# The RG-LRU block of a hybrid trunk: the square of the decay is taken out of the input's factor, and z's tiles get five buffers

## The chip, the core and the metric

The kernel runs on one core of a Trainium2 chip. The core has four engines that compute: TensorE (PE in the profile; its weight loads are listed as PEld), VectorE (DVE), ScalarE (ACT) and GpSimd (POOL). A fifth, SyncE (SP), only issues transfers here. Transfers run on 16 DMA engines and are issued from the queues of SP, ACT and POOL, each of which works in order. The metric is the device time of one execution in microseconds (us); lower is better.

## What is computed

Two layers of a trunk with 512 latent tokens and 256 context tokens, all in float32. The change lies in layer 0, whose mixer has two halves: SSD heads (Mamba-2) and RG-LRU blocks. The part of the reference that matters is the RG-LRU scan, which is done for two directions and eight blocks of 128 channels:

```python
def rglru_scan(u, h0, w_a, b_a, w_i, b_i, lam):
    r = jax.nn.sigmoid(jnp.einsum("btnk,nkj->btnj", u, w_a) + b_a)
    i = jax.nn.sigmoid(jnp.einsum("btnk,nkj->btnj", u, w_i) + b_i)
    log_a = -LRU_C * jax.nn.softplus(-lam) * r
    a = jnp.exp(log_a)
    bx = jnp.sqrt(-jnp.expm1(2 * log_a)) * (i * u)
    h = linear_recurrence(a, bx, h0)
    return h, h[:, -1]
...
y = rms_norm(y * jax.nn.silu(p["z"]), ssd_norm_g)
r = lru_h.reshape(bsz_, t, LRU_W) * jax.nn.gelu(p["gy"])
```

The factor sqrt(1 - a^2) is never formed from 1 - a^2 in the kernel. With c = 8 softplus(-lam), so that a = exp(-c r), the kernel before uses 1 - a^2 = (1 + a^2) tanh(c r), and the changed one uses 1 - a^2 = (1 + a)^2 tanh(c r / 2).

## The kernel before

Activations lie with channels on the 128 partitions and T = 768 tokens along the free dimension, context first. Every projection is done in three passes on TensorE, with weights and inputs split into a high and a low part: ScalarE writes the high part of a weight panel (`whi`, in `whalf`, L185 to L193), VectorE the low part (`wlo`, L193), in two halves of a panel.

The change touches one stage, `lru_phase` (L1236 to L1335). It works through eight blocks n of 128 channels. For each n there are these steps, written as a generator in an order of its own (L1316 to L1321):

- `proj_u(n)` (L1239): the projection of u, 24 matmuls of 512 columns into a `px` tile and 24 of 256 columns into a `pc` tile; then a causal convolution (`conv1d`), one tap on ScalarE and three on VectorE, and the split of the result into `uhi` and `ulo`.
- `proj_g(n)` (L1252): the projection of the output gate, in the same form, and a GELU on ScalarE that reads `px` and `pc` and writes `ge`.
- `gates(n)` (L1262): four products with 128x128 weights (`ghi`, `glo`) and a sigmoid each, which ScalarE writes into four tiles of the tag `gate` (four buffers): r and i for the two directions.
- `recur(n)` (L1285): for both directions a = exp(-c r) into `la_`, tanh(c r) in place; then the square of a into a tile `a2` that has one buffer, and (1 + a^2) tanh on VectorE (L1298); then the square root on ScalarE, two products, and the scan over time on VectorE (L1306 to L1309). The products i u (L1302) and the sum of the directions (L1311) run on GpSimd. The product with `ge` (L1312) is VectorE's, and the result goes out to `r_d`.
- `z_panel(n // 2)` for odd n (L1223): 256 columns of z. Six chunks of 128 tokens, each of 24 matmuls of 256 columns into a tile `pz`, which has the tag and the two buffers of `pc`. ScalarE copies `pz` to `zt`, which has two buffers, and issues the transfer of `zt` to `z_d`.

Between the steps run two other strands: the SSD scan (`ssd_phase`; its tiles are `bc`, `xw`, `yi`, `pyi`, `pin`, `pst`, `pcbm`), and the modulation vectors of later layers (`mod_tick`: tiles `mst` and `macc`, products on VectorE). The order in which each engine issues its instructions is not that of the program's text alone: the framework that the kernel is written in orders them over all engines from the dependences and its own estimates, so an edit can move instructions that it does not name.

ScalarE holds one table of functions at a time; where the next function needs another, an `ACT_TABLE_LOAD` stands in its queue.

Of the kernel before, what the change touches and what calls it, by code (L numbers as in the profile page):

```python
# [9 lines left out]
F32 = mybir.dt.float32  # L10
F32R = mybir.dt.float32r
AF = mybir.ActivationFunctionType
ALU = mybir.AluOpType
# [4 lines left out]
T = 768  # L18
# [46 lines left out]
def build(tc, I, out, dbg=None):  # L65
    nc = tc.nc
    V, S, G, PE, SP = nc.vector, nc.scalar, nc.gpsimd, nc.tensor, nc.sync
    if dbg is not None and "wrap" in dbg:
        V, S, G, PE, SP = [dbg["wrap"](e, n) for e, n in ((V, "V"), (S, "S"), (G, "G"), (PE, "PE"), (SP, "SP"))]
# [9 lines left out]
    def act(o, i, f, bias=0.0, scale=1.0, **kw):  # L79
        return S.activation(o, i, f, bias=bias, scale=scale, **kw)  # L80

    def stt(o, a, s, b, op0, op1, eng=None):
        return (eng or V).scalar_tensor_tensor(o, a, s, b, op0=op0, op1=op1)  # L83
# [5 lines left out]
    def psc(name="pc", n=256):  # L89
        return pp.tile([128, n], F32, tag="pc", name=name, bufs=2)  # L90
# [4 lines left out]
    def dump(name, ap):  # L95
        if dbg is not None and name in dbg:
            SP.dma_start(dbg[name], ap)
# [76 lines left out]
    def PS(n, i, k):  # L174
        q = POFF[n] + i
        assert q // 128 == (q + k - 1) // 128
        return PAR[q // 128][:, q % 128:q % 128 + k]
# [25 lines left out]
    def wpanel(W, r0, kt, c0, n, gain=None, byk=False, eng=None):  # L203
        return wsplit(wload(W, r0, kt, c0, n), kt, n, gain, byk, eng)
# [13 lines left out]
    def mm3s(o, hh, sl, w):  # L218

        for k in range(8):  # L220
            whi, wlo = w[k // 4]
            PE.matmul(o, hh[k][0][:, sl], whi[:, k % 4, :], start=(k == 0), stop=False)  # L222
            PE.matmul(o, hh[k][0][:, sl], wlo[:, k % 4, :], start=False, stop=False)  # L223
            PE.matmul(o, hh[k][1][:, sl], whi[:, k % 4, :], start=False, stop=(k == 7))  # L224
# [457 lines left out]
    def softplus_pos(dst, src, e, z, z2, p_):  # L682

        act(e, src, AF.Abs)
        act(e, e, AF.Exp, scale=-1.0)
        V.tensor_scalar(z, e, 2.0, None, op0=ALU.add)
        V.reciprocal(z, z)
        V.tensor_mul(z, z, e)
        V.tensor_mul(z2, z, z)
        V.tensor_scalar(p_, z2, 1.0 / 17, 1.0 / 15, op0=ALU.mult, op1=ALU.add)  # L690
        for m in (13, 11, 9, 7, 5, 3, 1):
            V.tensor_mul(p_, p_, z2)
            V.tensor_scalar(p_, p_, 1.0 / m, None, op0=ALU.add)
        V.tensor_mul(p_, p_, z)
        V.tensor_scalar(z2, src, 0.0, None, op0=ALU.max)
        stt(dst, p_, 2.0, z2, ALU.mult, ALU.add)
# [517 lines left out]
    c8 = ssc.tile([128, 16], F32, name="c8")  # L1214
    c8n = ssc.tile([128, 16], F32, name="c8n")
    with tc.tile_pool(name="c8p", bufs=1, reuse_waits="tile") as c8p:
        tt = [c8p.tile([128, 16], F32, name=f"c8t{i}") for i in range(5)]
        V.tensor_scalar(tt[4], PS("lam", 0, 16), -1.0, None, op0=ALU.mult)
        softplus_pos(c8, tt[4], tt[0], tt[1], tt[2], tt[3])
        V.tensor_scalar(c8n, c8, -8.0, None, op0=ALU.mult)  # L1220
        V.tensor_scalar(c8, c8, 8.0, None, op0=ALU.mult)

    def z_panel(lp, pb):  # L1223

        w = wpanel(W0, 0, 8, pb * 256, 256, byk=True, eng=G if KG[4] else V)
        for c in range(6):
            ps = psc("pz")
            cs = slice(c * 128, (c + 1) * 128)
            mm3s(ps, h, cs, w)
            zt = lp.tile([128, 256], F32, tag="zt", name="zt", bufs=2)  # L1230
            act(zt, ps, AF.Copy)
            S.dma_start(z_d[c, :, pb * 256:(pb + 1) * 256], zt)
            if c % 2:
                yield

    def lru_phase(lp):  # L1236
# [48 lines left out]
        def recur(n, u, gate):  # L1285
            hs, as_ = [], []
            for d in range(2):
                r_ = gate[d]
                ci = d * 8 + n
                a_ = lp.tile([128, T], F32, tag="la", name="la_", bufs=2)  # L1290
                act(a_, r_, AF.Exp, scale=c8n[:, ci:ci + 1])
                act(r_, r_, AF.Tanh, scale=c8[:, ci:ci + 1])
                as_.append(a_)
            for d in range(2):
                r_, a_ = gate[d], as_[d]
                a2 = lp.tile([128, T], F32, tag="la2", name="a2", bufs=1)
                act(a2, a_, AF.Square)
                stt(r_, a2, 1.0, r_, ALU.add, ALU.mult)  # L1298
            for d in range(2):
                r_, i_, a_ = gate[d], gate[2 + d], as_[d]  # L1300
                act(r_, r_, AF.Sqrt)
                (G, V)[d < KG[15]].tensor_mul(i_, i_, u)  # L1302
                (V, G)[d < KG[14]].tensor_mul(i_, i_, r_)
                h_ = r_
                if d == 0:
                    V.tensor_tensor_scan(h_, a_, i_, 0.0, op0=ALU.mult, op1=ALU.add)  # L1306
                else:
                    V.tensor_tensor_scan(h_[:, 0:256][:, ::-1], a_[:, 0:256][:, ::-1], i_[:, 0:256][:, ::-1], 0.0, op0=ALU.mult, op1=ALU.add)
                    V.tensor_tensor_scan(h_[:, 256:768][:, ::-1], a_[:, 256:768][:, ::-1], i_[:, 256:768][:, ::-1], h_[:, 0:1], op0=ALU.mult, op1=ALU.add)  # L1309
                hs.append(h_)  # L1310
            (V, G)[KG[0]].tensor_add(hs[0], hs[0], hs[1])  # L1311
            (V, G)[KG[1]].tensor_mul(hs[0], hs[0], GE.pop(n))  # L1312
            SP.dma_start(r_d[n], hs[0])
            dump(f"r_{n}", hs[0])
# [7 lines left out]
        for s_, n in order:  # L1322
            if s_ == "u":
                proj_u(n)
                yield
            elif s_ == "g":
                proj_g(n)
            elif s_ == "c":
                g_ = gates(n)
                yield  # L1330
                recur(n, *g_)
                yield
            else:
                yield from z_panel(lp, n // 2)
# [778 lines left out]
```

## Time and profile before

| | |
|---|---|
| time, median of 3 runs | 2139.82 us (2135.62 to 2142.2) |
| the profiled execution's own time | 2138.01 us |
| span from first to last instruction in it | 2136.3 us |
| mean granted TensorE clock | 0.975 of full speed |
| PE busy | 2022.4 us, 95% of the span |
| DVE busy | 1571.1 us, 74% |
| ACT busy | 872.8 us, 41% |
| POOL busy | 273.0 us, 13% |
| the stage of the RG-LRU | from about 240 to 560 us |

The profile gives times in us from the span's start. A row of a timeline has the start, the duration, the engine, the line of the kernel, the operation, the tiles written and read, and in brackets how long the engine stood idle just before and what released it. Helpers record many operations at one line: L80 is any activation, L83 any scalar_tensor_tensor, L215 any matmul of a projection. A table of windows gives for each stretch the busy time of the engines, and as PEclk the clock that TensorE was granted (1.00 is 2.4 GHz, 0.50 is 1.2 GHz).

### The profile page before, as it was taken

To read this page: it belongs to the slowest core of one execution; us is meant where nothing else is said; L and a number is where in the kernel's file an instruction comes from. 1 tells how busy PE (TensorE), PEld (TensorE's weight loads), DVE (VectorE), ACT (ScalarE), POOL (GpSimd) and SP (SyncE) were. 2 spreads that over 40 slices of the span, in tenths; PEclk is the share of its full clock that TensorE was granted. 3 is DMA by queue.
4 is the path that set the end of the run, shared out by engine and by line. 5 is a ranking of instruction groups with operands and counts; after the bars stand their busy time and mean duration, and the time that the engine had idled before them with its cause. 6 is when DMAs were issued, how large, how long until landed. Compare 5 with 4: busy or idle time off the path is not lost.

```text
span 2136.3 us, 32686 instructions
## 1 busy us (share of the span) xinstructions
PE 2022.4 (95%) x12738; PEld 1699.5 (80%) x12738; DVE 1571.1 (74%) x2916; ACT 872.8 (41%) x1276; POOL 273.0 (13%) x234
## 2 busy tenths in 40 slices
PE   8969989898898999999999999999999899999998
PEld 4848778787677888888888888897877688888887
DVE  5898898767778888868765656656876678667484
ACT  4625577586533442212321323324444344223234
POOL 2142333344421000000000000110011100000000
PEclk9979899999999999999999999999999999999999
DMA  9437535435676322333234112554421123222321
GB/s 332 132 102 206 152 98 168 123 97 165 225 242 215 99 87 94 112 121 116 94 118 139 62 50 94 152 160 147 126 71 58 40 80 99 97 82 98 99 84 55
DMA packets 283019, 261.09 MB, mean 122 GB/s; under 512 B 23406, under 2 KB 263061, under 8 KB 282865
## 3 DMA queue, kind: packets, MB, share of 16 engines
q1 hardware_dynamic: 257504, 243.35, 35.8%
q10 hardware_dynamic: 24464, 13.75, 2.3%
q8 instruction: 100, 1.64, 0.3%
q0 software_dynamic: 896, 1.90, 0.2%
q14 instruction: 55, 0.44, 0.1%
HBM read 224.17 MB, written 34.78 MB: 121 GB/s over the span
## 4 chain that ended last, share of the span: by engine, by line
PE 62%; DVE 6%; DMA 4%; POOL 1%; issue 1%; ACT 1%; SPq 0%; POOLq 0%; DVEq 0%; ACTq 0%
PE px L215 34%; PE pc L215 10%; PE pu L215 6%; PE pseg L215 4%; DMA mst<-in_w_mod_dram 1%; DVE macc L83 1%; PE pmodt L352 1%; PE pv L222 1%; PE pv L223 1%; PE pv L224 1%; POOL kc L1816 1%; PE plv L1858 1%; PE pob L215 1%; DMA xt<-xtok_d 0%; PE py L1711 0%
## 5 line engine op out<-in xcount | busy, mean ns | idle before, releaser
L80 ACT ACTIVATE whi<-st 128x1024 fp32r<-128x1024 f32 (+1 forms) x197 | 203.4, 1037 | 565.3 <-PE pc L215 365.1
L215 PE MATMUL px<-HH,whi 128*128 128x512 f32 (+2 forms) x1016 | 407.8, 403 | 15.3 <-DVE xbct L83 7.9
L215 PE MATMUL px<-HH,wlo 128*128 128x512 f32 (+2 forms) x1016 | 404.4, 398 | 0.0
L215 PE MATMUL px<-HL,whi 128*128 128x512 f32 (+2 forms) x1016 | 403.4, 397 | 0.9 <-DVE HL L83 0.9
L193 DVE TENSOR_TENSOR wlo<-st,whi 128x1024 fp32r<-128x1024 f32 (+1 forms) x197 | 237.5, 1209 | 78.3 <-ACT whi L80 76.3
L83 DVE SCALAR_TENSOR_TENSOR macc<-mst,sc,macc 128x256 f32<-128x256 f32 x434 | 216.9, 530 | 65.9 <-DMA mst<-in_w_mod_dram 64.8
L83 DVE SCALAR_TENSOR_TENSOR fa<-px,par,fa 128x441 f32<-128x441 f32 (+2 forms) x352 | 241.8, 691 | 8.2 <-ACT fa L80 2.2
L215 PEld LDWEIGHTS px<-HH,whi 128*128 128x128 f32 (+1 forms) x1016 | 192.0, 189 | 59.5 <-issue 9.6
L215 PEld LDWEIGHTS px<-HL,whi 128*128 128x128 f32 (+1 forms) x1016 | 191.8, 189 | 44.5 <-DVE HL L83 1.9
L215 PEld LDWEIGHTS px<-HH,wlo 128*128 128x128 f32 (+1 forms) x1016 | 191.8, 189 | 43.7
L215 PE MATMUL pc<-HH,whi 128*128 128x256 f32 x728 | 207.2, 286 | 4.6 <-ACT ge L80 3.2
L215 PE MATMUL pc<-HH,wlo 128*128 128x256 f32 x728 | 206.9, 285 | 0.0
L215 PE MATMUL pc<-HL,whi 128*128 128x256 f32 x728 | 206.9, 285 | 0.0
L215 PEld LDWEIGHTS pc<-HH,whi 128*128 128x128 f32 x728 | 137.8, 190 | 8.0 <-ACT ge L80 4.0
L80 ACT ACT_TABLE_LOAD x104 | 133.4, 1283 | 19.2 <-issue 5.4
L215 PEld LDWEIGHTS pc<-HL,whi 128*128 128x128 f32 x728 | 138.2, 190 | 1.1
L215 PEld LDWEIGHTS pc<-HH,wlo 128*128 128x128 f32 x728 | 138.2, 190 | 0.5
L215 PE MATMUL px<-fhi,wlo 128*128 128x512 f32 x304 | 120.4, 396 | 0.0
L215 PE MATMUL px<-fhi,whi 128*128 128x512 f32 x304 | 120.3, 396 | 0.0
L215 PE MATMUL px<-flo,whi 128*128 128x512 f32 x304 | 119.8, 394 | 0.0
L1815 POOL TENSOR_TENSOR kc<-kc,e 128x255 f32<-128x255 f32 x6 | 7.1, 1181 | 853.0 <-ACT kc L80 675.6
L215 PE MATMUL pu<-HH,wlo 128*128 128x512 f32 (+1 forms) x192 | 74.3, 387 | 0.0
(645 smaller groups left out, 4291.1 us busy)
## 6 DMA issues: line engine op xcount, KB each, us to landing
mst<-in_w_mod_dram SPq DMA_DIRECT2D x312, 128.0 KB, 2.2
st<-in_ffn_w_gate_dram SPq DMA_DIRECT2D x22, 1024.0 KB, 5.0
st<-in_ffn_w_up_dram SPq DMA_DIRECT2D x22, 1024.0 KB, 5.0
st<-in_ev_w_in_dram SPq DMA_DIRECT2D x18, 1024.0 KB, 6.4
st<-in_ffn_w_down_dram SPq DMA_DIRECT2D x16, 1024.0 KB, 5.0
bc<-cum_d SPq DMA_DIRECT2D x24, 512.0 KB, 6.2
sth<-in_od_w_in_dram SPq DMA_DIRECT2D x24, 512.0 KB, 4.0
st<-in_w_mod_dram SPq DMA_DIRECT2D x9, 1024.0 KB, 11.6
```

The source lines that it names most:

```text
L80: return S.activation(o, i, f, bias=bias, scale=scale, **kw)
L83: return (eng or V).scalar_tensor_tensor(o, a, s, b, op0=op0, op1=op1)
L193: (eng or V).tensor_sub(lo, src, hi.bitcast(F32))
L215: PE.matmul(o, ww[:, k, :M], hh[k][part][:, sl], start=(first and q == 0 and a == 0), stop=(stop and q == last and a == 2))
L222: PE.matmul(o, hh[k][0][:, sl], whi[:, k % 4, :], start=(k == 0), stop=False)
L223: PE.matmul(o, hh[k][0][:, sl], wlo[:, k % 4, :], start=False, stop=False)
L224: PE.matmul(o, hh[k][1][:, sl], whi[:, k % 4, :], start=False, stop=(k == 7))
L352: PE.matmul(pt[:, 2 * h_ + e:2 * h_ + e + 1], acc[:, e, h_ * 128:(h_ + 1) * 128], ones[:, 0:1], start=True, stop=True)
L1815: G.tensor_mul(kc[:, 0, 0:255], kc[:, 0, 0:255], e0[:, 0:255])
L1816: G.tensor_mul(kc[:, 1, 1:256], kc[:, 1, 1:256], e1[:, 1:256])
L1858: PE.matmul(v3[r:r + 32, c, :], kk(j), qq(j), start=True, stop=True, tile_position=(0, r))
```

## The change

The square and its tile go; the constant in the tanh is halved; the square root is taken of the tanh alone, and VectorE multiplies by (1 + a) after it, not before. Apart from that `zt` gets five buffers. The freed tile `a2` has 768 columns, the three added buffers of `zt` have 256 each.

```diff
@@ -1218,7 +1218,7 @@
         V.tensor_scalar(c8n, c8, -8.0, None, op0=ALU.mult)
-        V.tensor_scalar(c8, c8, 8.0, None, op0=ALU.mult)
+        V.tensor_scalar(c8, c8, 4.0, None, op0=ALU.mult)
@@ -1227,7 +1227,7 @@
-            zt = lp.tile([128, 256], F32, tag="zt", name="zt", bufs=2)
+            zt = lp.tile([128, 256], F32, tag="zt", name="zt", bufs=5)
@@ -1291,14 +1291,12 @@
                 act(r_, r_, AF.Tanh, scale=c8[:, ci:ci + 1])
                 as_.append(a_)
+
             for d in range(2):
-                r_, a_ = gate[d], as_[d]
-                a2 = lp.tile([128, T], F32, tag="la2", name="a2", bufs=1)
-                act(a2, a_, AF.Square)
-                stt(r_, a2, 1.0, r_, ALU.add, ALU.mult)
+                act(gate[d], gate[d], AF.Sqrt)
             for d in range(2):
                 r_, i_, a_ = gate[d], gate[2 + d], as_[d]
-                act(r_, r_, AF.Sqrt)
+                stt(r_, a_, 1.0, r_, ALU.add, ALU.mult)
                 (G, V)[d < KG[15]].tensor_mul(i_, i_, u)
                 (V, G)[d < KG[14]].tensor_mul(i_, i_, r_)
```

The edit moves instructions on every engine within this stage. In all, ScalarE has 16 activations fewer and 113 table loads where it had 104. Three places show how.

**First place: ScalarE, block n = 1, from the second exp to the GELU's second half** (a gate tile with the operand `c` is the tanh; with no other operand it is the square root; `a` is the tile of the square). Before:

```order
L80 ACTIVATE la__2852<-gate_2820,c8n 128x768
L80 ACTIVATE a_2855<-la__2849 128x768
L80 ACTIVATE gate_2820<-gate_2820,c_2332 128x768
L80 ACT_TABLE_LOAD
L80 ACTIVATE ge<-px 128x512
L80 ACTIVATE a_2858<-la__2852 128x768
L80 ACT_TABLE_LOAD
L80 ACTIVATE gate_2809<-gate_2809 128x768
L80 ACTIVATE gate_2820<-gate_2820 128x768
L80 ACT_TABLE_LOAD
L80 ACTIVATE ge<-pc 128x256
L80 ACTIVATE whi<-st 128x1024
```

Now:

```order
L80 ACTIVATE la__2848<-gate_2816,c8n 128x768
L80 ACT_TABLE_LOAD
L80 ACTIVATE gate_2805<-gate_2805 128x768
L80 ACT_TABLE_LOAD
L80 ACTIVATE gate_2816<-gate_2816,c_2332 128x768
L80 ACT_TABLE_LOAD
L80 ACTIVATE ge<-px 128x512
L80 ACT_TABLE_LOAD
L80 ACTIVATE gate_2816<-gate_2816 128x768
L80 ACT_TABLE_LOAD
L80 ACTIVATE ge<-pc 128x256
L80 ACTIVATE whi<-st 128x1024 x2
```

Both squares are gone, two table loads have come in, and both halves of z's weights (`whi`) now stand behind the GELU, where before only the second did. It is the same for n = 3 and 5. For even n the new order is exp, exp, tanh, tanh, table load, square root, square root, with no table load more than before.

**Second place: VectorE, the same block, from the factor to the low parts of z's weights.** Before:

```order
L83 SCALAR_TENSOR_TENSOR gate_2809<-a_2855,gate_2809 128x768
L83 SCALAR_TENSOR_TENSOR macc<-mst,sc,macc 128x256 x4
L83 SCALAR_TENSOR_TENSOR gate_2820<-a_2858,gate_2820 128x768
L1303 TENSOR_TENSOR gate_2831<-gate_2831,gate_2809 128x768
L1303 TENSOR_TENSOR gate_2842<-gate_2842,gate_2820 128x768
L1306 SCALAR_TENSOR_TENSOR gate_2809<-la__2849,gate_2831 128x768
L1308 SCALAR_TENSOR_TENSOR gate_2820<-la__2852,gate_2842 128x256
L1081 TENSOR_TENSOR hs_2091<-hs_2091,pst 128x512
L1309 SCALAR_TENSOR_TENSOR gate_2820<-la__2852,gate_2820,gate_2842 128x512
L193 TENSOR_TENSOR wlo<-st,whi 128x1024
L1312 TENSOR_TENSOR gate_2809<-gate_2809,ge 128x768
```

Now:

```order
L1304 SCALAR_TENSOR_TENSOR gate_2805<-la__2845,gate_2827 128x768
L83 SCALAR_TENSOR_TENSOR macc<-mst,sc,macc 128x256 x3
L83 SCALAR_TENSOR_TENSOR gate_2816<-la__2848,gate_2816 128x768
L1081 TENSOR_TENSOR hs_2091<-hs_2091,pst 128x512
L1301 TENSOR_TENSOR gate_2838<-gate_2838,gate_2816 128x768
L1127 TENSOR_TENSOR y<-y,pyi 128x512
L1306 SCALAR_TENSOR_TENSOR gate_2816<-la__2848,gate_2838 128x256
L193 TENSOR_TENSOR wlo<-st,whi 128x1024
L1307 SCALAR_TENSOR_TENSOR gate_2816<-la__2848,gate_2816,gate_2838 128x512
L193 TENSOR_TENSOR wlo<-st,whi 128x1024
```

The first direction's scan is now ahead of the second direction's factor, and both low parts of z's weights (`wlo`) stand between and behind the second direction's scans; before, the first of them was made one block of work earlier. The lines of the changed kernel from L1298 on are smaller by 2.

**Third place: TensorE, block n = 3, the start of the z panel.** Before, behind the last matmuls of the projection of g:

```order
L215 MATMUL px<-HH,wlo 128x512
L215 MATMUL pc<-HH,wlo 128x256
L222 MATMUL pz<-whi,HH 128x256
L223 MATMUL pz<-wlo,HH 128x256
L224 MATMUL pz<-whi,HL 128x256
```

Now the first matmuls of the panel stand here:

```order
L1126 MATMUL pyi<-xt,bc 128x64 x8
L352 MATMUL pmodt<-ones,macc 128x1 x4
L1100 MATMUL pcbm<-cch,bch 128x128
L222 MATMUL pz<-whi,HH 128x256 x2
L223 MATMUL pz<-wlo,HH 128x256
```

Before, twelve matmuls of the panel ran ahead of the 24 `px` matmuls of the next u, fourteen more behind them, and the other 118 as one run; now the 24 `px` matmuls, the `pyi`, `pmodt` and `pcbm` come first, and then all 144 of the panel in one run. It is the same for n = 1 and 5.

## Rows read from the trace of the kernel before

**Rows 1.** The page's first part: busy time, share of the span and instructions
```profile
PE 2022.4 (95%) x12738; PEld 1699.5 (80%) x12738; DVE 1571.1 (74%) x2916; ACT 872.8 (41%) x1276; POOL 273.0 (13%) x234
```
**Rows 2.** Table of windows by stage: stretch, length, busy time (instructions), clock, DMA
```profile
core 0: us, PE busy (x) PEld busy (x) DVE busy (x) ACT busy (x) POOL busy (x), PEclk, DMA share, GB/s
...
240.00:400.00 160.00, 142.77 (x818) 123.72 (x816) 144.90 (x196) 115.38 (x151) 57.44 (x33) 0.93 0.38 116
400.00:560.00 160.00, 141.97 (x901) 124.94 (x901) 109.80 (x107) 110.00 (x149) 72.19 (x42) 0.94 0.47 148
560.00:2136.00 1576.00, 1528.61 (x9836) 1292.88 (x9835) 1116.58 (x2130) 537.64 (x813) 79.61 (x66) 0.99 0.34 109
```
**Rows 3.** Timeline of PE in the stage: seven of its idle stretches
```profile
295.65 0.80 PE L215 MATMUL px<-HH,whi 128*128 128x512 f32 x1 [4.77 <-DVE u L83]
...
317.92 0.38 PE L222 MATMUL pz<-whi,HH 128*128 128x256 f32 x1 [2.30 <-ACT ge L80]
...
396.28 0.58 PE L222 MATMUL pz<-whi,HH 128*128 128x256 f32 x1 [4.43 <-ACT ge L80]
...
422.50 0.39 PE L1277 MATMUL pc<-uhi,ghi 128*128 128x256 f32 x1 [1.60 <-ACT zt L80]
...
496.30 0.39 PE L1277 MATMUL pc<-uhi,ghi 128*128 128x256 f32 x1 [3.23 <-ACT zt L80]
...
521.76 0.46 PE L1100 MATMUL pcbm<-cch,bch 128*128 128x128 f32 x2 [2.47 <-DMA cch<-cch_d]
...
556.28 3.65 PE L1126 MATMUL pyi<-xt,bc 128*128 128x64 f32 x16 [4.50 <-issue]
```
**Rows 4.** Table of windows, PE alone, behind five of these: stretch, busy, clock
```profile
core 0: us, PE busy (x), PEclk, DMA share, GB/s
296.00:299.50 3.50, 3.50 (x12) 0.60 0.99 238
319.50:326.50 7.00, 7.00 (x32) 0.53 0.46 140
396.00:405.00 9.00, 8.72 (x38) 0.52 0.30 88
497.00:500.50 3.50, 3.50 (x9) 0.54 0.30 104
...
556.00:561.00 5.00, 4.72 (x18) 0.50 0.58 220
```
**Rows 5.** Timeline of ACT, block n = 1: tanh, table load, exp, second square, GELU
```profile
302.18 0.93 ACT L80 ACTIVATE gate<-gate,c 128x768 f32<-128x768 f32 x1
303.13 1.28 ACT L80 ACT_TABLE_LOAD   x1
304.42 0.94 ACT L80 ACTIVATE la__2852<-gate,c8n 128x768 f32<-128x768 f32 x1
...
312.25 0.85 ACT L80 ACTIVATE a<-la__2852 128x768 f32<-128x768 f32 x1 [3.41 <-DVE gate L83]
...
317.49 0.38 ACT L80 ACTIVATE ge<-pc 128x256 f32<-128x256 f32 x1
```
**Rows 6.** Waits of ACT from 240 to 560: waited for, us in total, times, longest
```profile
ACT zt L80 <- DMA z_d<-zt: 16.9, 5, 4.0
ACT a L80 <- DVE gate L83: 12.0, 3, 5.9
```
**Rows 7.** Tile of the square: the first and the last of its 16 activations
```profile
L80 ACT ACTIVATE a<-la__2635 x1: 834/834/834, 272.8 to 272.8; 128x768 f32<-128x768 f32 x1
...
L80 ACT ACTIVATE a<-la__4850 x1: 841/841/841, 540.9 to 540.9; 128x768 f32<-128x768 f32 x1
```
**Rows 8.** Groups of ACT instructions from 240 to 560: the table loads
```profile
L80 ACT ACT_TABLE_LOAD x47 | 60.3, 1283 | 3.4 <-DMA r_d<-gate 2.2 <-ACT zt L80 0.4
```
**Rows 9.** Timeline of DVE: a low part, and products and last scan of n = 6
```profile
321.18 1.20 DVE L193 TENSOR_TENSOR wlo<-st,whi 128x1024 fp32r<-128x1024 f32 x1
...
516.05 3.25 DVE L1303 TENSOR_TENSOR gate<-gate,gate 128x768 f32<-128x768 f32 x2
...
523.70 1.27 DVE L1309 TENSOR_TENSOR_SCAN gate<-la__4707,gate,gate 128x512 f32<-128x512 f32 x1
```

## Prediction

> **What bounds the kernel now.** I began with the busy line of the page [rows 1]: TensorE works for 95% of the span, so the end is set by its matmuls. The edit changes none of them, so it can only win or lose time in which TensorE stands still or runs at a low clock. The table of windows says where that is [rows 2]. From 560 us on TensorE is busy for 1528.61 of 1576 us at clock 0.99; nothing is left there, and whatever this stage saves or loses is carried to the end as a shift. From 240 to 560 us it is busy for 142.77 and 141.97 of 160 us, so it idles 35.3 us, and with clocks of 0.93 and 0.94 it gives up to another 160 x 0.07 + 160 x 0.06 = 20.8 us to the clock. The edit cannot bring back more than these 56 us.
>
> The timeline of TensorE tells what it waits for there [rows 3]; the brackets are the idle time. Four places matter. It waits for u, the convolution on VectorE, at even blocks (4.77 us at 295.65). It waits for `ge` at the start of the z panels of n = 1 and 3 (2.30 and 4.43). It waits for `zt` at the end of those panels (1.60 and 3.23). At the end of the stage it waits twice more (2.47 and 4.50). Behind such a gap the clock is near its lower level of 1.2 GHz for a while: 0.60, 0.53, 0.52, 0.54 and 0.50 in the stretches behind five of them [rows 4]. A gap therefore costs its own length and then the stretch times the missing share of the clock.
>
> **The change, part by part.**
>
> *ScalarE's own work.* The 16 squares go, each between 834 and 841 ns [rows 7]: -13.4 us. Nine table loads come in at 1283 ns [rows 8]: +11.5 us. Net -1.9 us on an engine that is busy for 115 and 110 of 160 us [rows 2]. I cost this at nothing: TensorE's own work covers it, and without that cover it would be these 1.9 us. What counts is the order.
>
> *A, the old wait at the start of a z panel.* TensorE waited there for the second half of the GELU, since that frees the tile that the panel writes. In the order of ScalarE [rows 5] that half (317.49) stood behind the second square, which idled 3.41 us for VectorE's factor because both directions share one tile; all three such waits sum to 12.0 us [rows 6]. With the squares gone the GELU waits for no factor. The gaps of 2.30 and 4.43 go, and the slow clock behind them, 7.0 x 0.47 = 3.3 and 9.0 x 0.48 = 4.3 [rows 4]: -14.3 us. A is safe only if nothing else is late at the same place, which is B.
>
> *B, what is late next there.* Both halves of z's high parts now stand behind the GELU, and both low parts stand behind VectorE's scans. On ScalarE the second exp of n = 1 started at 304.42 [rows 5]. Behind it the new order has five table loads (5 x 1.28), two square roots (I take a square's 0.84 for each), a tanh (0.93) and the halves of a GELU (0.38, and twice that for twice the columns). With the exp itself (0.94) the GELU ends at about 315.5; a high part (as long as a low part at most, 1.20 [rows 9]) would end by 316.7, and its low part by 317.9. TensorE was free at 317.92 - 2.30 = 315.62 [rows 3], and now comes to the panel earlier by twelve matmuls; at the mean of 0.155 us (1528.61 / 9836 [rows 2]) that is at most 1.9 us, so at about 314. It waits 2 to 4 us; I take 3.5, with 3.5 x 0.46 = 1.6 of slow clock as behind the 3.23 us gap [rows 4]: 5.1 us for each of n = 1, 3 and 5, about +16. Its bounds: 0, if exp and tanh start as much earlier as the missing waits allow; +20, if each gap is as long as the longest in the list, 4.77, with the 1.4 to 1.75 us of clock that stand behind such a gap (3.5 x 0.40 and 3.5 x 0.5).
>
> *C, five buffers for `zt`.* ScalarE waited 16.9 us in five waits, 4.0 at most, for z's transfers to leave a `zt` [rows 6], and TensorE waited for ScalarE to empty the panel's tile: 1.60 and 3.23 us [rows 3]. With five buffers six chunks rarely meet a full set. -1.60 - 3.23 and 1.6 us of clock behind the second: -6.4 us. The other bound is 0, if ScalarE is held at that place by something else than the buffer. No buffer costs time of itself, and the transfers stay the same.
>
> *D, even blocks.* There the change adds no table load, and two squares (1.7 us) with one handover to the factor, which I take as another square's length, leave the chain from sigmoid to scan, behind which VectorE does the next convolution. For n = 0 the gap of 4.77 shrinks by 2.4 and its slow stretch (3.5 x 0.40 = 1.4) goes: -3.8. For n = 2 and 4, whose gaps are smaller, -1 each. -5.8 us; ends 0 (VectorE is late for its other strands) and -7.
>
> *E, the end of the stage.* Of n = 6 the two products at 516.05 took 3.25 us and the last scan ended at 523.70 + 1.27 [rows 9]; n = 7 needs these tiles. TensorE's gaps there are 2.47 and 4.50, the second with 5 x 0.5 = 2.5 us of clock. A chain shorter by two squares takes some of this: -3 us; ends 0 and -9.5, all of it.
>
> **Sum:** -14.3 + 16 - 6.4 - 5.8 - 3 = -13.5 us. The profiled execution took 2138.01 us (its span, 2136.3, and 1.7 around it), which gives 2124.5; the median of the runs shown, 2139.82, lies 1.8 higher, so the forecast is 2126. A difference under 0.3%, 6.4 us, cannot be told from none.
>
> With the terms at their ends: B at 0 and D, E at their lower ends would give -14.3 + 0 - 6.4 - 7 - 9.5 = -37; that all hold together I don't believe, since what frees TensorE at one gap makes it arrive earlier at the next. Half of the way, about 2113, is my lower end for this case; its upper end, with C at 0 and E at 0 and the rest as taken, is about 2136.
>
> **Rivals.**
>
> *No change.* B at +20 against A, with C as taken and D and E at 0: -14.3 + 20 - 6.4 = -0.7, about 2139. For it speaks that the chain of ScalarE is filled from 302 to 318 but for one wait [rows 5], and that wait is replaced by three table loads of 1.28. Against it, the transfers' waits are real and their removal is in the diff.
>
> *Slower, by VectorE.* The low parts stand now behind and between scans and products. In the trace of before one of them started at 321.18 [rows 9], when the scans were done. If VectorE reaches its scans no earlier than before, the first low part lands at 322.4, 8 us behind TensorE's arrival at 314; with a slow stretch as behind the 4.43 us gap (4.3) that is 12 us for each of n = 1, 3 and 5: -14.3 + 37 - 6.4 - 5.8 - 3 = +7.5, and about +10 if D gives half: 2147 to 2150. It decides once the first low part lands over 5 us behind the last `pyi` before the panel. For it: VectorE is busy for 144.90 of the first 160 us [rows 2], with the modulation's `macc` in line. Against it: nothing before the scans waits for squares any more.
>
> *Slower or the same, by ScalarE's table switches.* The tanh at 302.18 ends at 303.11, the load starts at 303.13 and the exp at 304.42 [rows 5]: 1.30 us for a switch and no pause beside it. If a switch cost twice that, nine more would take 23.4 against 13.4 us saved, ScalarE's chain in B would be 5 x 1.3 = 6.5 us longer in each odd block, and the result about 2126 + 3 x 4 = 2138. The Trainium skill, "ScalarE: Activation LUTs", sections "What ACT_TABLE_LOAD costs" and "Table sets: the hidden batching unit", speaks for this case: it puts a switch at 1283 ns and a drain of about 1380 ns, 2.66 us, and advises to keep functions of one set together, which the new order of odd blocks (exp, root, tanh, GELU, root, GELU) does not. The row bears out the load and no drain, so I go by the row and give this little.
>
> **How the numbers follow.** The forecast's case 0.55, no change 0.22, the table switches 0.05, slower by VectorE 0.18. Of the forecast's case some 0.03 lies within 0.3%: faster 0.52, same 0.28 (0.22 + 0.05 with the 0.03, less 0.02 for the no-change case ending above), slower 0.20. For 8 in 10, the lower end stays at 2113; upward the range takes in no change and switches and the lower edge of the slower case: 2148.
>
> **What would show it.** A: no activation waits for VectorE's factor, and `ge` no longer ends a gap at a z panel. B: at the start of the panels of n = 1, 3 and 5 a gap of 2 to 4 us that a `whi` or `wlo` ends; over 5 us is the slower rival. C: no `zt` waits for `z_d`, and no gap before the matmuls behind the panel. D: the gap before the `px` matmuls of even blocks at 2 to 3 us. Table loads at 1.28 us with no idle time beside them; if it stands there, the rule was right. The stage should be done some 13 us earlier, the rest as long as before, at clock 0.99. The forecast is wrong if that stage keeps its 35 us of idle time, or if the rest changes its length.

## The result, and the profile after

The changed kernel takes 2153.58 us (median of 4 runs, 2152.77 to 2157.22); the kernel before, run beside it on the same chip, 2141.01 us. The ratio is 1.0062, with a 95% interval of 1.0039 to 1.0084: slower by 0.6%, some 13 us, where the forecast was 2126 and the range ended at 2148. The profiled execution has a span of 2151.2 us.

The page's first part of the changed kernel, which answers to [rows 1]:

```profile
PE 2032.4 (94%) x12738; PEld 1707.2 (79%) x12738; DVE 1567.9 (73%) x2916; ACT 872.6 (41%) x1269; POOL 278.0 (13%) x234
```

The instructions are those that the diff promises. ScalarE's busy time is the same to 0.2 us (872.8 and 872.6): 16 squares went, nine table loads came, and seven entries fewer are left. The table of windows over the same stretches, as in [rows 2]:

```profile
core 0: us, PE busy (x) PEld busy (x) DVE busy (x) ACT busy (x) POOL busy (x), PEclk, DMA share, GB/s
240.00:400.00 160.00, 143.28 (x815) 123.49 (x813) 137.39 (x190) 108.86 (x139) 58.37 (x33) 0.93 0.40 124
400.00:560.00 160.00, 139.52 (x869) 122.65 (x868) 109.77 (x112) 111.06 (x147) 72.18 (x40) 0.93 0.42 132
560.00:2151.20 1591.20, 1540.73 (x9898) 1304.27 (x9896) 1124.56 (x2138) 542.85 (x821) 85.52 (x68) 0.99 0.34 110
```

Up to 560 us TensorE has got through fewer matmuls (869 in the second stretch, before 901); what is left over is done behind 560 us, at clock 0.99 as before. The stage ends later and carries the rest with it.

To measure the stage alone I use one length in every trace below: from the start of the first matmul of the gates of n = 0 to the start of the last matmul of z. Before it is 551.50 - 261.45 = 290.1 us; after, 565.09 - 266.95 = 298.1, so 8.1 us longer. The other 5.5 us were lost ahead of 266.95, where all engines still issue the same instructions in the same order. That part varies from profile to profile, as the last section shows, and I put it down to no cause. The stage alone, before and after (length, TensorE's busy time, granted clock):

```profile
261.45:551.50 290.05, 262.46 (x1609) 0.95 0.43 132
266.95:565.09 298.14, 265.98 (x1610) 0.93 0.41 129
```

So of the 8.1 us some 4.6 are idle time (27.6 and 32.2), and 3.5 are longer busy time for the same matmuls, at a lower clock.

TensorE's idle stretches in the changed kernel, to be read beside [rows 3]:

```profile
300.67 0.58 PE L1277 MATMUL pc<-uhi,ghi 128*128 128x256 f32 x1 [4.63 <-DVE u L83]
...
325.67 0.59 PE L352 MATMUL pmodt<-ones,macc 128*128 128x1 f32 x2 [4.17 <-DVE hs L1081]
...
405.94 0.37 PE L352 MATMUL pmodt<-ones,macc 128*128 128x1 f32 x1 [5.69 <-DVE yi L1088]
...
488.64 0.39 PE L223 MATMUL pz<-wlo,HH 128*128 128x256 f32 x1 [1.88 <-DVE wlo L193]
...
504.52 0.39 PE L222 MATMUL pz<-whi,HH 128*128 128x256 f32 x1 [3.48 <-ACT zt L80]
...
570.32 0.45 PE L1126 MATMUL pyi<-xt,bc 128*128 128x64 f32 x1 [4.95 <-issue]
```

The waits on `ge` at the panels of n = 1 and 3 (2.30 and 4.43) are gone, and longer ones stand in their place, 4.17 and 5.69, on two results of VectorE, `hs` and `yi`. The wait at 488.64, in the panel of n = 5, is on a low part of z's weights. VectorE's timeline ahead of the first of them:

```profile
306.93 6.46 DVE L83 SCALAR_TENSOR_TENSOR macc<-mst,sc,macc 128x256 f32<-128x256 f32 x4
...
318.69 0.95 DVE L83 SCALAR_TENSOR_TENSOR gate<-la__2845,gate 128x768 f32<-128x768 f32 x1
...
324.06 0.96 DVE L83 SCALAR_TENSOR_TENSOR gate<-la__2848,gate 128x768 f32<-128x768 f32 x1
324.93 0.69 DVE L1081 TENSOR_TENSOR hs<-hs,pst 128x512 f32<-128x512 f32 x1
...
327.59 1.20 DVE L193 TENSOR_TENSOR wlo<-st,whi 128x1024 fp32r<-128x1024 f32 x1
```

Both factors, with (1 + a), now stand behind their roots, at 318.69 and 324.06, and `hs` and `wlo` behind them. What VectorE's factor waits for from 240 to 560 us, before and after:

```profile
DVE gate L83 <- ACT a L80: 22.3, 6, 7.8
```

```profile
DVE gate L83 <- ACT gate L80: 23.1, 4, 8.1
```

What ScalarE's `zt` still waits for, and what stands in front of one of the last `zt` of n = 5:

```profile
ACT zt L80 <- DMA z_d<-zt: 2.4, 1, 2.4
```

```profile
503.14 1.06 ACT L80 ACTIVATE bc<-bc 128x1024 f32<-128x1024 f32 x1 [7.33 <-POOL bc L1109]
```

ScalarE's 12.0 us of waits on the factor [rows 6] are gone, but VectorE's waits on ScalarE are not: 22.3 us on the square before, 23.1 on the root now. The waits of `zt` on its buffers fell from 16.9 to 2.4 us. So both waits that the forecast counted on went, and neither bought time.

### The profile page after: what moved, and what is told of

It is laid out like the page before. It is cut to its first block, busy times and chain, and to the rows that moved or that the text cites. A ratio compares the mean times of both kernels' runs of the same rounds, so it can differ in the third digit from the quotient of the medians.

```text
span 2151.2 us, 32663 instructions
## 1 busy us (share of the span) xinstructions
PE 2032.4 (94%) x12738; PEld 1707.2 (79%) x12738; DVE 1567.9 (73%) x2916; ACT 872.6 (41%) x1269; POOL 278.0 (13%) x234
## 4 chain that ended last, share of the span: by engine, by line
PE 70%; DVE 15%; DMA 5%; issue 4%; ACT 3%; POOL 3%; SPq 0%; DVEq 0%; POOLq 0%; ACTq 0%
PE px L215 35%; PE pc L215 12%; PE pu L215 6%; PE pseg L215 4%; DMA mst<-in_w_mod_dram 3%; DVE macc L83 3%; PE pmod L298 1%; ACT L80 1%; DVE wlo L193 1%; ACT gate L80 1%; DVE xbct L83 1%; PE pmodt L352 1%; DVE bc L1107 1%; PE pv L222 1%; PE pv L223 1%
```

## The experiments

Because the scheduler moves instructions at every edit, most of the kernels hold an order by force. For that a function is called behind `build`, with a table that names, for each queue, the instructions of this stage by their place in the program's text:

```python
for e, text in table.items():
    seq = [...]   # the stage's instructions of queue e, in the order wanted
    for p, q in zip(seq, seq[1:]):
        tc.add_manual_dep(q, p.name, info, reason="pin")   # order of issue only, no wait
```

All ratios are to the kernel before, run beside each, so runs of different rows are best compared by them. The stage is the length defined above, from one profile of each; it can differ from what the times say by some us.

| run | formula, factor | order | zt | median us | ratio (95%) | stage us |
|---|---|---|---|---|---|---|
| before | old, ahead of root | before | 2 | | | 290.1 |
| changed | new, behind root | changed | 5 | 2153.58 | 1.0062 (1.0039 to 1.0084) | 298.1 |
| e1 | new, behind root | before | 5 | 2148.47 | 1.0034 (1.0017 to 1.0052) | 300.6 |
| e2 | new, behind root | before | 2 | 2153.10 | 1.0050 (1.0033 to 1.0067) | 299.7 |
| e3 | new, behind root | changed | 2 | 2151.72 | 1.0043 (1.0029 to 1.0056) | 298.3 |
| e4 | as changed | low parts first | 5 | 2161.08 | 1.0089 (1.0074 to 1.0104) | 308.2 |
| e5 | new, on i u | before | 5 | 2139.48 | 0.9994 (0.9980 to 1.0008) | 286.1 |
| e6 | new, on i u | free | 5 | 2145.86 | 1.0014 (1.0003 to 1.0024) | 287.3 |
| e7 | as changed | tables grouped | 5 | 2154.97 | 1.0056 (1.0039 to 1.0073) | 299.8 |
| e8 | old without squares | free | 2 | 2158.52 | one run | 280.5 |
| e9 | as e5 | six moves | 5 | 2137.81 | 0.9986 (0.9971 to 1.0001) | 289.0 |
| e10 | as e5 | six moves | 2 | 2136.75 | 0.9979 (0.9961 to 0.9996) | 284.2 |
| e11 | old | six moves | 2 | 2146.37 | 1.0019 (1.0004 to 1.0034) | 295.7 |
| e12 | old without squares | before | 2 | 2141.83 | 0.9996 (0.9983 to 1.0009) | 289.1 |
| e13 | new, on i u | changed, factors of odd n earlier | 5 | 2144.46 | 1.0006 (0.9990 to 1.0023) | 292.9 |
| e14 | as changed | macc later | 5 | 2159.74 | 1.0082 (1.0057 to 1.0108) | 308.2 |

### Is it the order? (e1, e2, e3)

The edit of e1 is the table alone: the changed kernel, in the order of the kernel before less its 16 squares.

> The changed kernel (new formula, five buffers) with the instructions of this stage held, on all five queues, in the order of the kernel before, less the 16 squares. Theory O (the order that the scheduler now picks costs the time, the formula itself saves): faster than before, by the old waits that go: the two GELU stalls with their slow clock (14 us) and the waits for the transfers of zt (6 us), so 2120 to 2130 us, and the z panels of n = 1 and 3 start without a wait for ge. Theory F (the formula itself costs: the root now stands ahead of the factor, and VectorE gets it later): 2145 to 2155 us, with VectorE's factor waiting for ScalarE by over 3 us in each block.

2148.47 us, ratio 1.0034: slower than before in the same order. Theory O falls, and F holds, though VectorE's factor waits for ScalarE at five places (38.9 us), not in each block. Where the time goes is plain in block n = 4. ScalarE's first tanh, VectorE's factor, its first product, and the last step of the next convolution, in the kernel before:

```profile
433.30 1.75 ACT L80 ACTIVATE gate<-gate,c 128x768 f32<-128x768 f32 x2
...
435.81 0.96 DVE L83 SCALAR_TENSOR_TENSOR gate<-a,gate 128x768 f32<-128x768 f32 x1 [7.80 <-ACT a L80]
...
440.24 1.83 DVE L1303 TENSOR_TENSOR gate<-gate,gate 128x768 f32<-128x768 f32 x2 [0.86 <-ACT gate L80]
...
453.26 0.47 DVE L83 SCALAR_TENSOR_TENSOR u<-pc,par,u 128x254 f32<-128x254 f32 x1
```

and in e1, with TensorE's wait behind it:

```profile
435.60 1.75 ACT L80 ACTIVATE gate<-gate,c 128x768 f32<-128x768 f32 x2
...
441.01 0.96 DVE L83 SCALAR_TENSOR_TENSOR gate<-la__4017,gate 128x768 f32<-128x768 f32 x1 [10.70 <-ACT gate L80]
...
444.49 1.82 DVE L1301 TENSOR_TENSOR gate<-gate,gate 128x768 f32<-128x768 f32 x2
...
458.29 0.47 DVE L83 SCALAR_TENSOR_TENSOR u<-pc,par,u 128x254 f32<-128x254 f32 x1
...
458.82 0.58 PE L1277 MATMUL pc<-uhi,ghi 128*128 128x256 f32 x1 [4.31 <-DVE u L83]
```

From the tanh to the first product it took 6.9 us before and takes 8.9 now; to the last step of the convolution 20.0 and 22.7. VectorE's queue stands 10.70 us at the factor (7.80 before, for the square), since the root that it now reads comes last on ScalarE, and whatever is behind it in the queue stands too.

e2 and e3 are e1 and the changed kernel with one figure changed:

```diff
-            zt = lp.tile([128, 256], F32, tag="zt", name="zt", bufs=5)
+            zt = lp.tile([128, 256], F32, tag="zt", name="zt", bufs=2)
```

> The same as the run before it, but zt has two buffers as in the kernel before. Theory B (the buffers carry a part of the gain, some 6 us, since ScalarE waits for z's transfers): 5 to 8 us slower than the five buffers, with waits of zt for z_d of 10 us or more in all. Rival (the buffers do nothing for the time, since ScalarE has time to spare): within 3 us of the five buffers, with the waits there or not.

> The changed kernel with two buffers for zt instead of five; the order of its instructions is that of the changed kernel on every engine. Theory B: slower than the changed kernel by 5 to 8 us, so 2158 to 2162 us, with waits of zt for z_d of 10 us or more. Rival (TensorE waits for VectorE before each panel, so a wait behind it costs little, or the five buffers cost something): 2150 to 2155 us.

Neither pair tells the buffers apart: 1.0050 against 1.0034 in the old order and 1.0043 against 1.0062 in the new, with intervals that overlap and opposite signs, and stages that differ by 0.9 and 0.2 us. The 4.6 us between the medians of e1 and e2 lie between the two ranges that I gave. Waits of `zt` for z's transfers are there with two buffers (6.4 us in e2, 8.3 in e3 and, as shown, 2.4 with five), but no time that these runs can tell hangs on them.

### Do VectorE's queue or ScalarE's tables hold the panel? (e4, e7, e14)

e4 changes VectorE's order behind the first scan of n = 1, and likewise in n = 3 and 5:

```diff
-macc x3, factor, hs, product, y, scan, wlo, scan, wlo
+hs, y, wlo, wlo, macc x3, factor, product, scan, scan
```

> The changed kernel in its own order, but on VectorE, in n = 1, 3 and 5, four instructions are moved to just behind the first direction's scan: the one that frees the PSUM tile for TensorE's small products (hs or yi), the sum y + pyi, and both low parts of z's weights. Theory V (the panel waits for VectorE, whose queue has six other instructions ahead of the low parts): the panels of n = 1, 3 and 5 start 3 to 5 us sooner, 9 to 15 us in all, so 2138 to 2145 us. Rival A (ScalarE's added table loads make the high parts late): no gain over 3 us, because the high parts come as late as before: 2150 to 2155 us. Rival R (the second direction's scan, now later, holds up the next block): 2150 us or more with the panels starting sooner.

2161.08 us; by the ratios 6 us more than the changed kernel, with intervals that overlap a little, and a stage that is 10 us longer. The panel of n = 1 starts sooner, and those of n = 3 and 5 end later: VectorE reaches the products of `bc` late, GpSimd gets them late, and ScalarE's exp of `bc` stands in front of the last copies of z. ScalarE and TensorE at the end of the panel of n = 3:

```profile
428.40 1.06 ACT L80 ACTIVATE bc<-bc 128x1024 f32<-128x1024 f32 x1 [10.55 <-POOL bc L1109]
...
429.78 0.58 PE L222 MATMUL pz<-whi,HH 128*128 128x256 f32 x1 [6.75 <-ACT zt L80]
```

Theory V falls as it was put (pulling these few instructions forward gains nothing); the mechanism is nearest to rival R, with another strand.

> The changed kernel in its own order, but on ScalarE, in n = 1, 3 and 5, tanh, both roots and both halves of the GELU stand in this order, so that nine table loads go (104 in all). Theory A (ScalarE's chain of table loads makes z's weights and the roots late): z's high parts come 3 us sooner in each of the three blocks and the time falls by 6 us or more, to 2142 to 2147 us. Rival V (VectorE's queue sets the start of the panel, and ScalarE's loads lie beside it): within 3 us of the changed kernel, 2150 to 2156 us.

ScalarE's order in the odd blocks, behind the second exp (| is a table load):

```diff
-| root | tanh | ge | root | ge
+tanh | root root | ge ge
```

Nine loads go, and the time stays (2154.97). In n = 1 the high parts are made at 313.73 us, 9.5 us behind the last sigmoid at 304.25, where the changed kernel needed 13.6 (321.81 and 308.18), and `hs` comes no sooner:

```profile
313.73 2.00 ACT L80 ACTIVATE whi<-st 128x1024 fp32r<-128x1024 f32 x2
```

```profile
322.20 0.68 DVE L1081 TENSOR_TENSOR hs<-hs,pst 128x512 f32<-128x512 f32 x1
```

That is 17.95 us behind the sigmoid, in the changed kernel 16.75. Theory A falls: the table loads lie beside VectorE's work.

> The changed kernel with its factor behind the root and its own order, but on VectorE the modulation products (macc) that stand between the first factor and the low parts, six in n = 1 and four in n = 3, are moved behind the second low part. Rival O (those products in front of hs, yi and the low parts are what holds the panels): hs and yi come 2 to 3 us sooner, the panels of n = 1 and 3 too, and the time falls by 4 us or more, to 2144 to 2150 us. Theory T: at most 3 us are gained, 2150 to 2156 us, since the factor stays where it is in all eight blocks.

2159.74 us. TensorE's waits at the panels fell to 1.84 (`hs`) and 2.62 us (`yi`), and three of 6.25, 7.86 and 4.49 us for `zt` stand at their ends. As in e4, what is put off on VectorE is waited for elsewhere. Rival O falls, and the time is above theory T's range too. The interval overlaps that of the changed kernel; the stage is 10 us longer.

### Where does the factor stand? (e5, e6, e13)

All three multiply i u by (1 + a), ahead of the root and not behind it; the instructions are as many:

```diff
             for d in range(2):
+                i_ = gate[2 + d]
+                (G, V)[d < KG[15]].tensor_mul(i_, i_, u)
+                stt(i_, as_[d], 1.0, i_, ALU.add, ALU.mult)
                 act(gate[d], gate[d], AF.Sqrt)
             for d in range(2):
                 r_, i_, a_ = gate[d], gate[2 + d], as_[d]
-                stt(r_, a_, 1.0, r_, ALU.add, ALU.mult)
-                (G, V)[d < KG[15]].tensor_mul(i_, i_, u)
```

> The new formula with five buffers, in the order of the kernel before less the squares, as in the first run; but VectorE multiplies by (1 + a) not the square root of the tanh but i u, ahead of the root. The number of instructions is the same. Theory T (the changed formula puts VectorE's factor behind ScalarE's root, so both factors, 0.95 us each, stand in the chain from the last sigmoid to the next convolution and to z's low parts; before they were done while ScalarE was busy): faster than the first run by 8 us or more, and than the kernel before: 2128 to 2138 us; VectorE's factor waits for ScalarE for under 10 us in all. Rival N (the place of the factor does not matter, the first run lost its time to the clock and to other strands): within 4 us of the first run, 2144 to 2152 us.

2139.48 us, ratio 0.9994: 9 us below e1, with intervals that do not touch, though 1.5 us above the end of the range that I gave, and not told apart from the kernel before. VectorE's factor waits for ScalarE for 9.4 us in all. In n = 4:

```profile
433.43 1.20 DVE L83 SCALAR_TENSOR_TENSOR gate<-la__4017,gate 128x768 f32<-128x768 f32 x1 [4.67 <-ACT la__4017 L80]
434.06 1.75 ACT L80 ACTIVATE gate<-gate,c 128x768 f32<-128x768 f32 x2
...
439.47 1.83 DVE L1302 TENSOR_TENSOR gate<-gate,gate 128x768 f32<-128x768 f32 x2
...
452.49 0.47 DVE L83 SCALAR_TENSOR_TENSOR u<-pc,par,u 128x254 f32<-128x254 f32 x1
```

The first factor starts ahead of the tanh; from the tanh to the first product it is 5.4 us (e1 8.9), to the end of the convolution 18.4 (e1 22.7). The stage of the one profile is 14.5 us shorter than e1's, more than the medians say.

> The same formula as the run before it, with the factor on i u, and the scheduler left free to order the instructions. Theory T with the order as a second, separate cost: slower than the run before it but faster than the changed kernel, 2138 to 2148 us. Rival N: 2150 us or more.

2145.86 us, as expected: about 8 us below the changed kernel (10 by the ratios), with the scheduler free.

> The changed kernel's own order, held on all queues, with the factor on i u as in the fifth run; on VectorE both factors of n = 1, 3 and 5 are moved up to just behind the last bc ahead of them, and nothing else is moved. Theory T (the factor's place costs the time, in any order): 2140 to 2147 us, as the sixth run, and the stage from the first gate to the last matmul of z 8 us or more shorter than the changed kernel's 298 us. Rival O (in the odd blocks the order costs it, and the sixth run was faster for the scheduler's order, not for the formula): 2150 to 2156 us and a stage of 295 us or more.

2144.46 us, ratio 1.0006 against the changed kernel's 1.0062; the intervals do not touch, so the factor's place costs time in this order too, about 9 us between the medians and 12 by the ratios, and theory T holds. The stage is 5.2 us shorter, not 8. The waits at the panels of n = 1 and 3 are still there (4.97 on `hs`, 5.89 on `yi`), so the factor's place does not make them. The one on `yi` is there in the old order as well (5.16 in e5, below); the one on `hs` belongs to the new order (0.87 in e5). The first gates of n = 4 start at 433.78 us in the changed kernel and at 429.50 in e13, those of n = 6 at 511.81 and 504.00: counted from the stage's start, 1.0 and 4.5 us sooner, so most of the gain came in n = 4 and 5. From the tanh to the last step of the convolution of n = 4, rows of the changed kernel and then of e13:

```profile
443.46 1.75 ACT L80 ACTIVATE gate<-gate,c 128x768 f32<-128x768 f32 x2
...
462.61 0.47 DVE L83 SCALAR_TENSOR_TENSOR u<-pc,par,u 128x254 f32<-128x254 f32 x1
```

```profile
439.17 1.75 ACT L80 ACTIVATE gate<-gate,c 128x768 f32<-128x768 f32 x2
...
456.58 0.48 DVE L83 SCALAR_TENSOR_TENSOR u<-pc,par,u 128x254 f32<-128x254 f32 x1
```

19.2 and 17.4 us: 1.7 less, about the two factors of 0.95 us.

### What are the squares worth? (e8, e12)

Both are the kernel before with the factor read from a, not from its square, so that their output is that of another function; the factor stays ahead of the root. e12 also holds the old order.

```diff
-                a2 = lp.tile([128, T], F32, tag="la2", name="a2", bufs=1)
-                act(a2, a_, AF.Square)
-                stt(r_, a2, 1.0, r_, ALU.add, ALU.mult)
+                stt(r_, a_, 1.0, r_, ALU.add, ALU.mult)
```

> The kernel before without its 16 squares and their tile: the factor reads a where it read the square of a, so the output is that of another function; the scheduler is free. It shows what the squares cost where the factor stays ahead of the root. Theory T: as fast as the kernel before or faster, 2125 to 2140 us. Rival N: 2145 us or more, since the squares' removal alone shakes the order.

One run, 2158.52 us, though the stage is the shortest of all, 280.5: rival N's figure. Behind the stage the SSD scan is left over: TensorE idles for it at 549.68 and 556.43 us (3.62 and 3.75), and at 578.63 for the high part of r (4.60). In this run an early end of z was worth nothing by itself, since what follows it took 1611.6 us, and 1584.8 before.

> The kernel before without its 16 squares and their tile (the factor reads a, so the output is that of another function), now with the instructions held in the order of the kernel before. Theory W: what the squares cost is small, since yi and the other waits take the place of theirs: 2135 to 2142 us, as the fifth run. Theory Q (the squares and the waits on their one tile are worth the 10 us or more that the prediction gave them): 2122 to 2131 us.

2141.83 us, ratio 0.9996. Theory Q falls. The gaps that were to go are still there, on TensorE:

```profile
319.71 0.38 PE L222 MATMUL pz<-whi,HH 128*128 128x256 f32 x1 [2.21 <-ACT ge L80]
...
396.12 0.58 PE L222 MATMUL pz<-whi,HH 128*128 128x256 f32 x1 [3.96 <-ACT ge L80]
```

and the reason stands on VectorE and ScalarE ahead of the first:

```profile
309.68 3.33 DVE L83 SCALAR_TENSOR_TENSOR macc<-mst,sc,macc 128x256 f32<-128x256 f32 x4
```

```profile
313.91 0.84 ACT L80 ACTIVATE gate<-gate 128x768 f32<-128x768 f32 x1 [2.48 <-DVE gate L83]
...
317.12 0.84 ACT L80 ACTIVATE gate<-gate 128x768 f32<-128x768 f32 x1 [2.37 <-DVE gate L83]
```

Without a square the root is the next to wait for VectorE's factor, which stands behind four products of the modulation.

### Can the gain be had? (e9, e10, e11)

In e5 TensorE still waits at the panel of n = 3 and at the ends of those of n = 3 and 5:

```profile
399.51 1.66 PE L352 MATMUL pmodt<-ones,macc 128*128 128x1 f32 x7 [5.16 <-DVE yi L1088]
...
423.25 0.39 PE L1277 MATMUL pc<-uhi,ghi 128*128 128x256 f32 x1 [1.96 <-ACT zt L80]
...
495.64 0.39 PE L1277 MATMUL pc<-uhi,ghi 128*128 128x256 f32 x1 [3.06 <-ACT zt L80]
```

Six instructions were moved ahead for these: VectorE's `yi` and second `wlo` of n = 3 to just behind the second factor, and ScalarE's last `zt` of n = 3 and 5, each with its transfer, ahead of the exps of `bc`.

> The kernel of the fifth run (factor on i u, old order, five buffers), with six moves in its queues: in n = 3, VectorE's yi and the second low part of z go ahead of the products and scans; at the end of the panels of n = 3 and 5, ScalarE's last zt and its transfer go ahead of the exps of bc. Theory W (what the change takes away at the panel, TensorE then waits for at yi and at zt, 5.2, 2.0 and 3.1 us in that run's trace, and the slow clock behind): faster than the fifth run by 8 to 12 us, 2127 to 2132 us, and clear of the kernel before. Rival S (those queues only pass the wait on, since the strand of the SSD scan or the modulation is late anyway): within 3 us of the fifth run, 2136 to 2143 us.

> The same kernel and order with two buffers for zt. Theory B (the buffers matter once ScalarE copies zt without waiting for bc): slower than the run before it by 4 us or more, with zt waiting for z_d for over 5 us. Rival (a copy and its transfer keep up with two): within 3 us.

> The kernel before, formula, squares and two buffers included, with the same six moves in its order. Theory W: the formula's gain shows only with the moves and the moves' gain only with the formula at n = 3, where the panel there waits for ge (4.43 us) and not for yi; at most zt's moves gain, 0 to 5 us: 2136 to 2142 us. Rival M (the moves alone make the gain, whatever the formula): as fast as the kernel with the moves and the new formula, within 3 us.

e9 gives 2137.81 us (0.9986, an interval that just reaches 1). The three waits did go, and others took their place: at the end of the panel of n = 3 a wait of 6.13 us for `zt`, and in n = 6 one of 4.25 for u. Rival S holds. With two buffers it is as fast or faster (0.9979), within the 3 us of the rival there, though `zt` waits for z's transfers again:

```profile
ACT zt L80 <- DMA z_d<-zt: 19.5, 8, 4.0
```

So 19.5 us of waiting on ScalarE costs nothing here. e11 is slower than before, above theory W's range, so the moves do nothing for the old formula; in its trace the same two waits came as in e9 (2.77 us at 417.15 for `zt`, 4.61 at 499.02 for u). That the moves help the new formula is not shown, since the intervals of e5, e9 and e10 overlap. e10 is the one version of fourteen whose interval lies below 1, at 0.9979; of the versions tried, the new formula with its factor on i u pays 0.2% at best.

## Why the prediction was wrong

The step that failed is one that is not there: no term of the sum costs the new place of the factor. The diff shows that `stt` moves from ahead of the root to behind it, and the second place of the order shows it on VectorE; I read it as part of a chain that becomes shorter, and D even books the handover to the factor as gone. Two multiplications of 0.95 us came to stand behind the root, in the chain from the last sigmoid to the next convolution, in each of eight blocks, 15 us if all of it counted. What the runs show is 9 us between the medians, in either order (e1 against e5, the changed kernel against e13); by the ratios it is 8.6 and 12, and the stages of single profiles say 14.5 and 5.2, so the sign is sure and the size only roughly known.

That is not the whole miss, which is 27.6 us. With the factor on i u the formula is as fast as the kernel before in either order (0.9994 and 1.0006), where the sum had -13.5 us. So, with B's cost set against them, the gains that were booked came to nothing as well; C and D fell furthest short. The rest, by its own steps:

- **What bounds the kernel.** Right. The stage lost 8.1 us, the rest behind it has the same clock and 1.3 us more (14.9 us of span less 5.5 and 8.1).
- **ScalarE's own work at nothing.** Right: busy 872.6 after 872.8, and nine loads less change nothing (e7). A switch is still 1.30 us with no pause beside it. The drain of about 1380 ns that the Trainium skill, "ScalarE: Activation LUTs", section "What ACT_TABLE_LOAD costs", adds to a load does not show in this case. In the changed kernel's ScalarE, behind a tanh that ends at 309.48:

```profile
309.50 1.28 ACT L80 ACT_TABLE_LOAD   x1
310.80 0.94 ACT L80 ACTIVATE la__2848<-gate,c8n 128x768 f32<-128x768 f32 x1
```

- **A, -14.3 us.** Right for the waits: `ge` ends no gap at a panel in the changed kernel, where the root waits for no factor. What took their place is B. The squares alone had not held `ge`: without them, but with the factor ahead of the root, both gaps stay at 2.21 and 3.96 us (e12), because the root then waits for VectorE's queue as the square did.
- **B, +16 us.** A new wait at the panels was forecast, 3.5 us by low parts; it is 4.17 and 5.69 us, by `hs` and `yi`, with the low part right behind, and 1.88 by a low part in n = 5. Place and sign were right and the size was close (though three times 5.1 is 15.3, not 16), but in n = 1 and 3 the cause was another. It was not the factor that made it: with the factor moved it stays (e13).
- **C, -6.4 us.** Wrong, the other bound of 0 was right. The waits for the transfers went from 16.9 to 2.4 us and the time did not follow (e2 and e3, e10 against e9): the last `zt` stand behind the exps of `bc`, which wait for GpSimd (7.33 us at 503.14). TensorE's waits of 1.60 and 3.23, which stand behind the panels of n = 3 and 5 and not of n = 1 and 3, are 0.88 and 3.48 at the ends of these panels now.
- **D and E, -8.8 us.** Wrong in size. The wait for u behind n = 0, of which 2.4 us were to go, is 4.63 after 4.77. The chain of n = 4 became shorter by 0.8 us (20.0 to 19.2), as two squares went and two factors came; with the factor off it, it is 17.4 (e13). At the end of the stage the wait for `cch` (2.47) is gone and the other stays (4.95 after 4.50).
- **The rivals.** The slower one came nearest: VectorE, in the odd blocks, with a time of 2147 to 2150. Its condition was met, since the first low part landed at 327.59 + 1.20 and the last `pyi` ended at 319.61 + 1.89, so 7.3 us apart. That the time came near it is in part luck, since its cause did not hold: pulling the low parts forward, or the modulation back, gained nothing (e4, e14).

What stays open is how much the new order costs by itself. The pairs (e1 and the changed kernel, e5 and e13) say 0.3 and 0.1%, with intervals that overlap; and in e8 an order alone seems to cost more than all else, from one run. Open too is how a place in the queue turns into 9 us: the chain was followed in n = 4 alone.

## What to carry to other kernels

When an algebraic change saves an operation, look where the operations that remain now stand: a factor that moves from ahead of the other engine's last step to behind it can come into the chain, though the number of operations is the same, and it belongs on an operand that is ready early (here i u). A wait that ends late in a queue is only the last of several; before its whole length is booked as a gain, find what the waiting instruction's next input would be. And where a scheduler orders the queues, hold the order fixed and change the arithmetic alone, or the two can't be told apart.

## What was not expected of the hardware

With the same instructions in the same order, the clock granted to TensorE can differ by a lot between two profiles. The windows from 140 to 160 us, well ahead of the stage, before (0.87) and after (0.58):

```profile
140.00:160.00 20.00, 16.58 (x110) 0.87 0.51 140
```

```profile
140.00:160.00 20.00, 18.00 (x94) 0.58 0.53 143
```

The first gate of n = 0 started between 258.8 and 267.0 us in the sixteen profiles. Differences of a few us between two profiles tell nothing there, which is why the table gives the stage apart from the time.

VectorE's multiply-adds stretch when GpSimd computes: four of `macc` took 6.46 us (306.93 above) while GpSimd was at work from 306.47 to 313.12; a single one at 318.29, with GpSimd idle, took 0.48. GpSimd's rows, and that of VectorE:

```profile
306.47 1.45 POOL L1116 TENSOR_TENSOR y<-xt,dbc 128x512 f32<-128x512 f32 x1 [0.68 <-DMA yp_d<-y]
307.87 1.28 POOL L1109 TENSOR_SCALAR_AFFINE_SELECT bc<-bc 128x1024 f32<-128x1024 f32 x1
309.12 4.00 POOL L1300 TENSOR_TENSOR gate<-gate,u 128x768 f32<-128x768 f32 x2
```

```profile
318.29 0.48 DVE L83 SCALAR_TENSOR_TENSOR macc<-mst,sc,macc 128x256 f32<-128x256 f32 x1 [1.35 <-DMA mst<-in_w_mod_dram]
```

The Trainium skill, "SBUF — State Buffer", section "SBUF: two separate sides", tells of a pair of ports which one of the two engines holds for a whole instruction; the rows agree with it, as far as durations can show it. What it costs here no run shows: VectorE then stood idle for 1.35 us, for a transfer, ahead of the `macc` at 318.29.
